# Five small edits in one diff to a two-layer network: where a row scale stands, which engine adds squares, how far apart sixteen mixing steps lie, and how weight blocks are added up

## The chip, the cores and the metric

The kernel runs on one core of a Trainium2 chip. A core has TensorE (PE, matrix products), VectorE (DVE), ScalarE (ACT), GpSimd (POOL), and SyncE (SP), which here only issues transfers; 16 DMA engines move data. ACT and POOL issue transfers as well. Each engine works through its own instructions in order and waits on semaphores for the others. The metric is device time in microseconds, the median of several executions. All arithmetic is float32: a product of two float32 matrices is made of three matmuls on a high and a low part of each operand (hi·hi, hi·lo, lo·hi), so each block of weights needs a cast (`whi`, on ACT) and a subtraction (`wlo`, on DVE) before TensorE can use it.

## The reference

512 tokens of width 2048 pass two layers. The first (forgetting attention and RWKV7) is untouched by the change. The part that matters:

```python
xn = rms_norm(h, norm_pre[1])
u, v, g = split(xn @ c_w_in[0], 3)          # 2048 x 6144
u = gelu(u); v = layer_norm(gelu(v), c_ln_g, c_ln_b)
# 16 groups of 128 channels, chunks of 128 tokens, w_s[g] is 128 x 128, lower triangle
mixed = einsum('gts,bnsgc->bntgc', w_s * causal, v_chunks) + b_s
y = (u * mixed * silu(g)) @ c_w_out[0]      # 2048 x 2048
h = h + rms_norm(y, norm_post[1])
h = h + (p[1] @ ple_w_proj[1]) * sigmoid(h @ ple_w_gate[1])   # the output
```

## The kernel before, in words

**Products of half blocks.** The large products of the second layer (`c_w_in`, `c_w_out`, the last `ple_w_gate`) are made by `seven`: a pair of column strips of 512 of W is cut into four blocks of 1024 x 512 (kh, ch), and a Strassen-like scheme makes the two strips from seven products in place of eight, each over sums of blocks. A product has eight steps k ("ticks", a counter that `tick` advances); at a step TensorE does six matmuls. `pieces` provides W's side: `load` is a plain transfer of 512 KB from SP's queue, `grow` an accumulating transfer of 512 KB from POOL's queue (it adds the block to a tile that lies in SBUF), `add` an addition on DVE (L1408). For product 4 a pair with `whole` uses `grow`; any other loads the block in half tiles of 256 KB from SP (L1445), into one of two buffers `half0`, `half1`, and adds each on DVE. `Pair` has no `whole` but the first pair of the last gate.

**Order.** For two pairs worked together (`FIRST`) the products run 1 and 2 of both, then 5, 6, 3, 4, 7 of the first, then 5, 6 and an `end` of the second: 3, 4, 7, or 4, 7, 3 in the last gate. The gating pairs of `c_w_in` go U0, G0, U1, G1, each in the order 1, 2, 5, 6, 3, 4, 7. When a product is finished, DVE combines the results (L1506 for product 3, L1519 and L1524 on for 7 and for 4 with 7) and `emit` gives each block of outputs to what follows. Work beside the products is put into a list with a due tick (`later`), and the program's order on each engine is mostly the order in which it is written, with priorities for some pieces (`high_priority`).

**Mixing.** After the values (V) and two products of a U pair, `mix` is started for eight groups, twice in all. For a group it puts into the list, relative to a tick `at`: at -11 the `load` (values `vn` and w_s, gains and shifts, from ACT's queue; the tiles are `sq`, `rstdB`, `accq`), at -4 the `norm` (ACT L1585 four times; POOL's triangle mask L1588; DVE), at 0 the `split` (a transpose on TensorE, casts L1597, L1600 and L1601), at 5 the `mul` (three matmuls L1607 on; one DVE operation on u). The group's `at` is 43 + 6.4 e for e = 0 to 7.

**c_w_out** (`last_layer`). Its outputs come in four blocks a pair; `out_block` scales each, squares it on ACT (L1141) and adds the square to `accq[e]` (L1143) for the row norm, e being the half of the tokens. Eight of these additions are on POOL and six on DVE. `row_scale(e)` (L1152, then ACT's table and L371 on) sums over partitions with TensorE and makes the row's scale; it has the highest priority. `row_scale(0)` is due in the second pair's last products, `row_scale(1)` after strip g = 0 of the following product.

**The last part.** The projection `p @ ple_w_proj` is made by `dense_tm` in four strips g of 24 matmuls; each strip's four results are copied by ACT (L1214) and parked in DRAM. Beside them `update` (L1200, L1201) adds the normed `c_w_out` result to h: half 0 in the loop, half 1 (`late`) from the first ticks of the gate's products on. Then `seven` for the gate, whose `emit` (ACT L1275, DVE L1276, L1278) makes the outputs.

Of the kernel before, what the change touches and what calls it, by code (L numbers as in the profile page):

```python
# [16 lines left out]
P = 128  # L17
# [78 lines left out]
class Pair:  # L96


    def __init__(self, W, c0, n, emit):
        self.W, self.c0, self.n, self.emit, self.whole = W, c0, n, emit, False  # L100
        self.E, self.H, self.acc, self.R, self.done = {}, {}, {}, {}, set()


class Net:
# [1017 lines left out]
    def last_layer(self, cp, fs, turn, wp, ps):  # L1122
# [8 lines left out]
        def out_block(pr, m, n, src):  # L1131
            e, q = m // 2, 2 * n + m % 2
            tl = self.slot("yh", 2 * q + e, F32) if q < 4 else self.slot("xl", 2 * q + e, F32)
            Y[q, e] = tl.rearrange("p (a t) -> p a t", a=2)
            sv = src.rearrange("p (a t) -> p a t", a=2)
            for a in range(2):
                c = 16 + 2 * q + a
                self.last = nc.scalar.activation(Y[q, e][:, a, :], sv[:, a, :], AF.Copy, scale=npost[:, c : c + 1])
            if seen[e]:
                sq = self.t(wp, [P, T], "sq")  # L1140
                nc.scalar.activation(sq, src, AF.Square)  # L1141
                eng = nc.vector if pr.n == 2 and n + e > 2 else nc.gpsimd
                eng.tensor_tensor(accq[e], accq[e], sq, ALU.add)  # L1143
            else:
                nc.scalar.activation(accq[e], src, AF.Square)
            seen[e] = True
# [60 lines left out]
        for g in range(4):  # L1207
            accs = self.dense_tm(i["ple_w_proj"][1], g * T, T, phi, plo, ps)
            for q in (g, g + 4):
                update(q, 0)  # L1210
            self.part(self.A11, g, H[g, 0])
            for m in range(4):
                pj = self.slot("xl", 4 * (g % 2) + m, F32)
                nc.scalar.copy(pj, accs[m])  # L1214
                nc.sync.dma_start(self.pd[:, m, g * T : (g + 1) * T], pj)
            x2(g)
            if g == 0:
                row_scale(1)

        pj, res = {}, {}  # L1220
# [62 lines left out]
        W = i["ple_w_gate"][1]  # L1283
        pairs = [Pair(W, 2 * j * T, 2 * j, emit) for j in range(2)]
        pairs[0].whole = True
        self.seven(FIRST(*pairs, (4, 7, 3)), Sets(nxt), ps)
        self.clock += 100
        self.tick()
# [100 lines left out]
    def pieces(self, pr, prod, keep):  # L1389
# [20 lines left out]
        for j in range(4):  # L1410
            done = None
            if prod == 1:
                tl = load(0, 0, j)
                if keep:
                    pr.E[j] = tl
                else:
                    done = tl
            elif prod == 5:
                if j not in pr.E:
                    pr.E[j] = load(0, 0, j)  # L1420
                tl = pr.E[j]
                grow(tl, 0, 1, j)
            elif prod == 2:
                tl = done = load(1, 0, j)
            elif prod == 6:
                pr.H[j] = load(1, 1, j)
                tl = pr.E[j]
                add(tl, pr.H[j])
            elif prod == 3:
                if j in pr.H:  # L1430
                    tl = pr.H[j]
                else:
                    tl = done = load(1, 1, j)
            elif prod == 7:
                tl = done = pr.H.pop(j)
                grow(tl, 0, 1, j)
            elif pr.whole:
                tl = done = pr.E.pop(j)
                grow(tl, 1, 0, j)
            else:  # L1440
                tl = done = pr.E.pop(j)
                for a in range(2):
                    g = self.t(self.wq, [P, T], f"half{a}")
                    k = 8 + 2 * j + a
                    nc.sync.dma_start(g, pr.W[k * P : (k + 1) * P, pr.c0 : pr.c0 + T])  # L1445
                    add(tl[:, a * T : (a + 1) * T], g)
# [11 lines left out]
    def seven(self, order, sets, ps, after=lambda n: None, fm=False):  # L1458
# [3 lines left out]
        for step, (pr, prod, keep) in enumerate(order):  # L1462
# [30 lines left out]
            for m in range(2):  # L1493
# [9 lines left out]
                    u2 = pr.R[1][:, m]  # L1503
                    nc.vector.tensor_tensor(u2, a, u2, ALU.add)
                elif prod == 3:
                    nc.vector.scalar_tensor_tensor(a, a, -1.0, pr.R[1][:, m], ALU.mult, ALU.subtract)  # L1506
                    pr.emit(pr, m, pr.n + 1, a)
            pr.done.add(prod)
            if prod == 7:
                u3 = pr.R[7] = pr.R[1] if 3 in pr.done else self.t(self.rp, [P, 2, T], "comb")  # L1510
                for m in range(2):
                    nc.vector.tensor_tensor(u3[:, m], acc[m], pr.R[1][:, m], ALU.add)
                    c22 = pr.R[5][:, m]
                    nc.vector.tensor_tensor(c22, c22, u3[:, m], ALU.add)
                    pr.emit(pr, 2 + m, pr.n + 1, c22)
            if prod in (4, 7) and {4, 7} <= pr.done:
                for m in range(2):
                    u = pr.R[7][:, m]
                    nc.vector.tensor_tensor(u, pr.acc[4][m], u, ALU.subtract)  # L1519
                    pr.emit(pr, 2 + m, pr.n, u)  # L1520
            after(step)

    def add_sq(self, accq, src, n, wp):
# [11 lines left out]
    def layer_c(self, cp, sets, accq, after, wp, ps):  # L1535
# [79 lines left out]
        V = [Pair(W, D + 2 * j * T, 2 * j, vals) for j in range(2)]  # L1615
        U = [Pair(W, 2 * j * T, 2 * j, gates) for j in range(2)]
        G = [Pair(W, 2 * D + 2 * j * T, 2 * j, silu) for j in range(2)]
        order = FIRST(*V)
        for pr in (U[0], G[0], U[1], G[1]):
            order += [(pr, prod, True) for prod in NEXT]  # L1620
# [30 lines left out]
        def done(step):  # L1651
# [20 lines left out]
            for j in range(2):  # L1672
                if step == nv + 14 * j + 1:
                    for e in range(8):
                        mix(8 * j + e, 5 * 8 + 3 + int(6.4 * e))
            if step == nv + 13:
                for n in range(2):
                    self.later(4, lambda n=n: saved(n))
# [290 lines left out]
```

## Time and profile before

| | us |
|---|---|
| median of 3 executions | 2251.96 (2250.07 to 2252.22) |
| the profiled execution, its own time | 2256.05 |
| its span (first to last instruction) | 2254.3 |
| TensorE busy in it | 2211.8 (98%) |
| VectorE busy | 1556.7 (69%) |
| ScalarE busy | 1274.5 (57%) |
| GpSimd busy | 264.1 (12%) |

The stages of the second layer by the trace's time: `c_w_in` until about 1885, its mixing near 1600 to 1680 and 1800 to 1860; `c_w_out` 1885 to 2045; the projection 2048 to 2079; the last gate from there to 2246, where TensorE's last matmul ends. In rows of the timeline the first number is the start, the second the duration, then engine, line, operation, output and inputs, shapes and count; brackets hold the idle time of that engine before the row and what ended it. In rows of waits the numbers are the total in us, how often, and the longest.

### The profile page before, as it was taken

How to read it: one execution, taken by the hardware profiler on the slowest of the kernel's cores; microseconds unless marked ns; L12 is line 12 of the kernel's file. 1: busy time of each engine (PE TensorE's matmuls, PEld its weight loads, DVE VectorE, ACT ScalarE, POOL GpSimd, SP SyncE). 2: the span in 40 equal slices, each digit the busy share in tenths (PEclk: the TensorE clock that was granted, in tenths of full speed). 3: DMA queues.
4: the chain of work that ended last, by engine and by line, in shares of the span. 5: the costliest groups of instructions: out<-in, count | busy, mean ns of one | idle time of the engine just before them, and what ended most of it. 6: DMA issues, size and time to landing. Idle time of an engine off the chain costs nothing.

```text
span 2254.3 us, 40541 instructions
## 1 busy us (share of the span) xinstructions
PE 2211.8 (98%) x15369; PEld 1839.4 (82%) x15369; DVE 1556.7 (69%) x3006; ACT 1274.5 (57%) x2597; POOL 264.1 (12%) x316
## 2 busy tenths in 40 slices
PE   8999999999999999999999999999999999998998
PEld 7878888888887788878888888888878879997876
DVE  8766667666633878883227356987787787989867
ACT  5545555555543677763335456656665667656744
POOL 2000010001100000000010012010110110220120
PEclk9999999999999999999999999999999999999999
DMA  7322232222324633343335345687866966577694
GB/s 235 92 79 70 74 87 82 66 76 76 85 75 116 193 103 99 103 117 129 96 103 163 121 131 143 171 212 195 214 170 181 225 177 167 137 192 246 169 260 141
DMA packets 294769, 313.79 MB, mean 139 GB/s; under 512 B 15101, under 2 KB 190878, under 8 KB 293550
## 3 DMA queue, kind: packets, MB, share of 16 engines
q1 hardware_dynamic: 249838, 253.52, 36.6%
q0 software_dynamic: 22848, 44.05, 11.3%
q10 hardware_dynamic: 21888, 13.64, 2.1%
q8 instruction: 121, 1.98, 0.4%
q14 instruction: 74, 0.61, 0.1%
HBM read 280.45 MB, written 30.70 MB: 138 GB/s over the span
## 4 chain that ended last, share of the span: by engine, by line
PE 78%; DVE 9%; DMA 6%; ACT 4%; issue 3%; SPq 0%; ACTq 0%; DVEq 0%; POOLq 0%
PE mm L1488 21%; PE mm L210 11%; PE mm L212 10%; PE mm L211 10%; PE mm L992 4%; PE mm L994 4%; PE mm L993 4%; DVE wlo L1453 3%; DMA sq<-vd 2%; PE tm L548 1%; ACT whi L1452 1%; DMA rq<-in_ple_w_gate_dram 1%; DVE rq L1408 1%; PE tm L569 1%; DMA gz<-gd 1%
## 5 line engine op out<-in xcount | busy, mean ns | idle before, releaser
L196 DVE TENSOR_TENSOR wlo<-raw,whi 128x512 fp32r<-128x512 f32 x400 | 283.5, 717 | 300.9 <-ACT whi L194 266.1
L194 ACT CAST whi<-raw 128x512 fp32r<-128x512 f32 x400 | 247.3, 619 | 349.0 <-PE mm L211 143.8
L211 PE MATMUL mm<-xl,whi 128*128 128x512 f32 x1056 | 414.5, 392 | 0.0
L210 PE MATMUL mm<-xh,whi 128*128 128x512 f32 x992 | 411.8, 415 | 0.0
L212 PE MATMUL mm<-xh,wlo 128*128 128x512 f32 x992 | 391.8, 395 | 0.0
L1452 ACT CAST whi<-rq 128x512 fp32r<-128x512 f32 x432 | 264.8, 620 | 194.1 <-PE mm L1488 120.5
L1453 DVE TENSOR_TENSOR wlo<-rq,whi 128x512 fp32r<-128x512 f32 x432 | 298.4, 700 | 103.0 <-ACT whi L1452 101.2
L211 PEld LDWEIGHTS mm<-xl,whi 128*128 128x128 f32 x1056 | 199.2, 189 | 32.4
L212 PEld LDWEIGHTS mm<-xh,wlo 128*128 128x128 f32 x992 | 186.2, 188 | 41.2
L210 PEld LDWEIGHTS mm<-xh,whi 128*128 128x128 f32 x992 | 186.9, 188 | 33.1
L1488 PE MATMUL mm<-whi,xl 128*128 128x512 f32 x512 | 165.6, 398 | 2.0 <-ACT whi L1452 1.7
L1488 PE MATMUL mm<-whi,yl 128*128 128x512 f32 x512 | 164.1, 394 | 0.4 <-ACT whi L1452 0.3
L1488 PE MATMUL mm<-whi,yh 128*128 128x512 f32 x512 | 161.4, 391 | 0.0
L1488 PEld LDWEIGHTS mm<-whi,xl 128*128 128x128 f32 x512 | 98.0, 191 | 23.5 <-ACT whi L1452 2.1
L1488 PEld LDWEIGHTS mm<-whi,yl 128*128 128x128 f32 x512 | 96.0, 188 | 21.2 <-ACT whi L1452 1.2
L1488 PEld LDWEIGHTS mm<-whi,yh 128*128 128x128 f32 x512 | 96.1, 188 | 20.2
L1453 DVE TENSOR_TENSOR wlo<-raw,whi 128x512 fp32r<-128x512 f32 x128 | 89.0, 697 | 33.6 <-ACT whi L1452 33.2
L1452 ACT CAST whi<-raw 128x512 fp32r<-128x512 f32 x128 | 78.5, 619 | 50.5 <-PE mm L1488 27.8
L1488 PE MATMUL mm<-wlo,xl 128*128 128x512 f32 x256 | 101.8, 398 | 3.0 <-DVE wlo L1453 3.0
L1488 PE MATMUL mm<-wlo,yl 128*128 128x512 f32 x256 | 100.5, 393 | 3.1 <-DVE wlo L1453 3.0
L1488 PE MATMUL mm<-wlo,yh 128*128 128x512 f32 x256 | 99.8, 390 | 0.0
L1488 PE MATMUL mm<-whi,xh 128*128 128x512 f32 x256 | 80.3, 390 | 0.0
(523 smaller groups left out, 4675.2 us busy)
## 6 DMA issues: line engine op xcount, KB each, us to landing
raw<-in_ab_w_in_dram SPq DMA_DIRECT2D x128, 512.0 KB, 3.9
rq<-in_c_w_in_dram SPq DMA_DIRECT2D x50, 512.0 KB, 5.0
raw<-in_ple_w_gate_dram SPq DMA_DIRECT2D x42, 512.0 KB, 3.9
rq<-in_c_w_in_dram POOLq DMA_DIRECT2D x36, 512.0 KB, 7.6
raw<-in_ab_w_out_dram SPq DMA_DIRECT2D x32, 512.0 KB, 3.8
raw<-in_c_w_in_dram SPq DMA_DIRECT2D x26, 512.0 KB, 5.1
half<-in_c_w_in_dram SPq DMA_DIRECT2D x48, 256.0 KB, 3.2
rq<-in_c_w_out_dram SPq DMA_DIRECT2D x24, 512.0 KB, 10.7
```

What stands on the lines that cost most here:

```text
L194: nc.scalar.copy(hi[:, : m * n], src)
L196: self.weng.tensor_tensor(lo[:, : m * n], src, f(hi[:, : m * n]), ALU.subtract)
L210: nc.tensor.matmul(acc, hi, xhi[k], start=(k == 0), stop=False)
L211: nc.tensor.matmul(acc, hi, xlo[k], start=False, stop=False)
L212: nc.tensor.matmul(acc, lo, xhi[k], start=False, stop=(k == nk - 1))
L548: nc.tensor.matmul(px[dst, e, :], a[src, e, :], b[src, e, :], start=True, stop=True)
L992: nc.tensor.matmul(accs[j], hi[:, js], xhi[k], start=(k == 0), stop=False)
L993: nc.tensor.matmul(accs[j], hi[:, js], xlo[k], start=False, stop=False)
L994: nc.tensor.matmul(accs[j], lo[:, js], xhi[k], start=False, stop=(k == nk - 1))
L1452: self.cast = nc.scalar.copy(hi, src)
L1453: nc.vector.tensor_tensor(lo, src, f(hi), ALU.subtract)
L1488: nc.tensor.matmul(o, x, y, start=(first and r == 0 and j == 0 and not a), stop=(r == 7 and j == 2), **more)
```

## The change

Line numbers of the changed kernel are one higher than before from line 101 on and 18 or 20 higher behind the combination code. The diff has six parts. `row_scale(1)` is asked for after strip 2 of the projection, not 0. All additions of squares in `out_block` go to DVE. The G pairs get `whole`: product 4's second block comes by four accumulating transfers of 512 KB a pair from POOL's queue, in place of eight half tiles and eight DVE additions. The mixing's ticks become 38 + 7.1 e. The last gate's second pair loads its half tiles into eight slots of `yl` that its product 5 has freed, in place of the two buffers. In `seven`, where product 3 is the last, products 4 and 7 are combined as each of them ends (two copies by ACT are new), and the operations on the last product's results get high priority.

```diff
@@ class Pair
-        self.W, self.c0, self.n, self.emit, self.whole = W, c0, n, emit, False
+        self.W, self.c0, self.n, self.emit = W, c0, n, emit
+        self.whole, self.half = False, None
@@ out_block
-                eng = nc.vector if pr.n == 2 and n + e > 2 else nc.gpsimd
-                eng.tensor_tensor(accq[e], accq[e], sq, ALU.add)
+                nc.vector.tensor_tensor(accq[e], accq[e], sq, ALU.add)
@@ last_layer
             x2(g)
-            if g == 0:
+            if g == 2:
                 row_scale(1)
@@ last_layer
         pairs[0].whole = True
+        pairs[1].half = lambda k: self.slot("yl", 8 + k, F32)
@@ pieces
                 for a in range(2):
-                    g = self.t(self.wq, [P, T], f"half{a}")
+                    g = pr.half(2 * j + a) if pr.half else self.t(self.wq, [P, T], f"half{a}")
@@ seven
                 elif prod == 3:
-                    nc.vector.scalar_tensor_tensor(a, a, -1.0, pr.R[1][:, m], ALU.mult, ALU.subtract)
-                    pr.emit(pr, m, pr.n + 1, a)
+                    with tc.high_priority(HP) if step == len(order) - 1 else nullcontext():
+                        nc.vector.scalar_tensor_tensor(a, a, -1.0, pr.R[1][:, m], ALU.mult, ALU.subtract)
+                        pr.emit(pr, m, pr.n + 1, a)
             pr.done.add(prod)
-            if prod == 7:
-                u3 = pr.R[7] = pr.R[1] if 3 in pr.done else self.t(self.rp, [P, 2, T], "comb")
+            if prod == 4 and 7 not in pr.done:
+                if 3 not in pr.done:
+                    for m in range(2):
+                        c22, u = pr.R[5][:, m], pr.R[1][:, m]
+                        nc.vector.tensor_tensor(c22, c22, u, ALU.add)
+                        nc.vector.tensor_tensor(acc[m], acc[m], u, ALU.subtract)
+            elif prod == 7 and 3 not in pr.done:
+                for m in range(2):
+                    c22 = pr.R[5][:, m]
+                    nc.vector.tensor_tensor(c22, acc[m], c22, ALU.add)
+                    pr.emit(pr, 2 + m, pr.n + 1, c22)
+                c21 = self.t(self.rp, [P, 2, T], "comb")
+                for m in range(2):
+                    nc.scalar.copy(c21[:, m], acc[m])
+                    nc.vector.tensor_tensor(c21[:, m], pr.acc[4][m], c21[:, m], ALU.subtract)
+                    pr.emit(pr, 2 + m, pr.n, c21[:, m])
+            elif prod == 7:
+                u3 = pr.R[7] = pr.R[1]
...
-            if prod in (4, 7) and {4, 7} <= pr.done:
-                for m in range(2):
-                    u = pr.R[7][:, m]
-                    nc.vector.tensor_tensor(u, pr.acc[4][m], u, ALU.subtract)
-                    pr.emit(pr, 2 + m, pr.n, u)
+                if 4 in pr.done:
+                    for m in range(2):
+                        u = u3[:, m]
+                        nc.vector.tensor_tensor(u, pr.acc[4][m], u, ALU.subtract)
+                        pr.emit(pr, 2 + m, pr.n, u)
@@ layer_c
         G = [Pair(W, 2 * D + 2 * j * T, 2 * j, silu) for j in range(2)]
+        for pr in G:
+            pr.whole = True
@@ layer_c
-                        mix(8 * j + e, 5 * 8 + 3 + int(6.4 * e))
+                        mix(8 * j + e, 38 + int(7.1 * e))
```

On TensorE, where the second row scale stands, before (`whi`, `wlo` are a weight block's parts, `yl` the operand's; each `mm` is a PSUM bank, and 22559 is the last bank of strip 0, 22622 and 22623 the first two of strip 1):

```order
L251 MATMUL mm_22559<-whi_22578,yl_4534_21951 128x512
L252 MATMUL mm_22559<-wlo_22579,yl_4534_21951 128x512
L253 MATMUL mm_22559<-whi_22578,yl_4535_21952 128x512
L1152 MATMUL mm_22616<-rstdB_12775,ones_118 128x256 x2
L251 MATMUL mm_22622<-whi_22628,yl_4530_21940 128x512
L252 MATMUL mm_22622<-wlo_22629,yl_4530_21940 128x512
L253 MATMUL mm_22622<-whi_22628,yl_4531_21941 128x512
L251 MATMUL mm_22623<-whi_22628,yl_4530_21940 128x512
```

and changed (22579 is the last bank of strip 1, 22636 to 22639 are the banks of strip 2):

```order
L253 MATMUL mm_22579<-wlo_22599,yl_4518_21911 128x512
L254 MATMUL mm_22579<-whi_22598,yl_4519_21912 128x512
L252 MATMUL mm_22636<-whi_22642,yl_4514_21900 128x512
L253 MATMUL mm_22636<-wlo_22643,yl_4514_21900 128x512
...
L252 MATMUL mm_22638<-whi_22642,yl_4514_21900 128x512
L253 MATMUL mm_22638<-wlo_22643,yl_4514_21900 128x512
L254 MATMUL mm_22638<-whi_22642,yl_4515_21901 128x512
L252 MATMUL mm_22639<-whi_22642,yl_4514_21900 128x512
L1152 MATMUL mm_22696<-rstdB_12775,ones_118 128x256 x2
L253 MATMUL mm_22639<-wlo_22643,yl_4514_21900 128x512
L254 MATMUL mm_22639<-whi_22642,yl_4515_21901 128x512
```

The row scale's two matmuls moved behind strip 1 and the first ten matmuls of strip 2.

On SP, the queue of plain transfers, in the second pair of the last gate, before (`rq` and `raw` are blocks of W of 512 KB, `out` the outputs):

```order
L1400 DMA rq_5010_24081<-in_ple_w_gate_dram 128x2x512
L1445 DMA half_5024_24137<-in_ple_w_gate_dram 128x512
L1445 DMA half_5025_24140<-in_ple_w_gate_dram 128x512
L1280 DMA out_dram<-yl_4874_23485 128x512
L1445 DMA half_5030_24163<-in_ple_w_gate_dram 128x512
L1445 DMA half_5031_24166<-in_ple_w_gate_dram 128x512
L1445 DMA half_5036_24189<-in_ple_w_gate_dram 128x512
L1445 DMA half_5037_24192<-in_ple_w_gate_dram 128x512
L1400 DMA rq_5061_24320<-in_ple_w_gate_dram 128x2x512
```

and changed:

```order
L1401 DMA rq_4994_24041<-in_ple_w_gate_dram 128x2x512
L1446 DMA yl_5001_24068<-in_ple_w_gate_dram 128x512
L1446 DMA yl_5002_24071<-in_ple_w_gate_dram 128x512
L1446 DMA yl_5008_24097<-in_ple_w_gate_dram 128x512
L1446 DMA yl_5009_24100<-in_ple_w_gate_dram 128x512
L1446 DMA yl_5014_24123<-in_ple_w_gate_dram 128x512
L1446 DMA yl_5015_24126<-in_ple_w_gate_dram 128x512
L1446 DMA yl_5020_24149<-in_ple_w_gate_dram 128x512
L1446 DMA yl_5021_24152<-in_ple_w_gate_dram 128x512
L1280 DMA out_dram<-yl_4858_23445 128x512
L1401 DMA rq_5045_24284<-in_ple_w_gate_dram 128x2x512
```

Eight loads now stand in one run into eight tiles, ahead of the output.

On POOL, in the first G pair, before (AFFINE_SELECT is the triangle mask of a group, here of e = 3 to 7 and of the second half's first; the transfers are those of product 7):

```order
L1588 AFFINE_SELECT accq_17942<-accq_17942 128x128
L1588 AFFINE_SELECT rstdB_12775<-rstdB_12775 128x128
L1588 AFFINE_SELECT accq_18139<-accq_18139 128x128
L1588 AFFINE_SELECT rstdB_12775<-rstdB_12775 128x128
L1404 DMA raw_18150<-in_c_w_in_dram 128x2x512
L1404 DMA raw_18173<-in_c_w_in_dram 128x2x512
L1404 DMA rq_3757_18210<-in_c_w_in_dram 128x2x512
L1588 AFFINE_SELECT accq_18324<-accq_18324 128x128
L1404 DMA rq_3763_18238<-in_c_w_in_dram 128x2x512
L1588 AFFINE_SELECT rstdB_12775<-rstdB_12775 128x128
```

and changed (masks of e = 3 to 7; the four `rq_36..` transfers behind the third mask are product 4's, the rest again product 7's):

```order
L1606 AFFINE_SELECT accq_17905<-accq_17905 128x128
L1606 AFFINE_SELECT rstdB_12775<-rstdB_12775 128x128
L1606 AFFINE_SELECT accq_18118<-accq_18118 128x128
L1405 DMA rq_3659_17784<-in_c_w_in_dram 128x2x512
L1405 DMA rq_3665_17818<-in_c_w_in_dram 128x2x512
L1405 DMA rq_3671_17845<-in_c_w_in_dram 128x2x512
L1405 DMA rq_3680_17876<-in_c_w_in_dram 128x2x512
L1405 DMA raw_18155<-in_c_w_in_dram 128x2x512
L1606 AFFINE_SELECT rstdB_12775<-rstdB_12775 128x128
L1405 DMA raw_18187<-in_c_w_in_dram 128x2x512
L1606 AFFINE_SELECT accq_18331<-accq_18331 128x128
L1405 DMA rq_3757_18210<-in_c_w_in_dram 128x2x512
```

Product 4's four transfers were added behind the mask of e = 5, and the masks of e = 6 and 7 now stand among product 7's transfers.

On DVE the last operations changed order: between the two subtractions of the last product 3 (L1506, now L1508) five other operations stood before, and two stand now.

## The prediction

> **What bounds the kernel now.** I began with the page's busy line, to see whether anything but TensorE can set the time, and then asked for TensorE's waits alone.
>
> ```profile
> span 2254.3 us, 40541 instructions
> PE 2211.8 (98%) x15369; PEld 1839.4 (82%) x15369; DVE 1556.7 (69%) x3006; ACT 1274.5 (57%) x2597; POOL 264.1 (12%) x316
> ```
>
> ```profile
> PE mm L1488 <- DVE wlo L1453: 10.2, 14, 2.3
> PE mm L1152 <- issue: 5.8, 1, 5.8
> PE mm L1607 <- DVE sg L1601: 2.4, 2, 1.9
> ```
>
> TensorE is busy for all but 42.5 us (2254.3 - 2211.8). The change keeps the count of matmuls, so it can win only idle time of TensorE, time in which its clock was lowered, and what follows the last matmul. The three rows hold 18.4 us of that idle time, and each is a place that the change touches. I then read these places one by one in the timeline and in windows of 4 us, where a window is: span, busy time of PE, PEld, DVE, ACT, POOL, granted clock, DMA share, GB/s. Everything else is layer A, which stays.
>
> **Part 1: the second row scale.** `row_scale(1)` (L1152) is queued on TensorE straight behind the first strip of the projection, and needs the last VectorE addition of squares (L1143).
>
> ```profile
> 2053.53 0.39 PE L252 MATMUL mm<-wlo,yl 128*128 128x512 f32 x1
> 2053.76 0.39 PE L253 MATMUL mm<-whi,yl 128*128 128x512 f32 x1
> 2059.97 2.04 PE L1152 MATMUL mm<-rstdB,ones 128*128 128x256 f32 x4 [5.83 <-issue]
> ```
>
> ```profile
> 2059.18 0.69 DVE L1143 TENSOR_TENSOR rstdB<-rstdB,sq 128x512 f32<-128x512 f32 x1
> ```
>
> ```profile
> 2059.06 2.03 ACT L1214 COPY xl<-mm 128x512 f32<-128x512 f32 x4
> ```
>
> ```profile
> 2056.00:2060.00 4.00, 0.03 (x1) 0.06 (x1) 3.99 (x8) 3.97 (x8) 0.00 (x0) 0.87 0.43 125
> 2060.00:2064.00 4.00, 4.00 (x10) 3.16 (x11) 3.96 (x7) 3.43 (x8) 0.00 (x0) 0.50 0.89 309
> 2064.00:2068.00 4.00, 4.00 (x15) 3.22 (x14) 3.34 (x7) 1.21 (x2) 0.00 (x0) 0.78 0.07 27
> ```
>
> The releaser "issue" is not the cause: the addition ended at 2059.87 and the matmul began at 2059.97. The stall is 5.83 us, and the clock behind it fell to 0.50 and 0.78: of these 8 us, 4 x 0.50 + 4 x 0.22 = 2.9 us are lost. At stake are 8.7 us. In the changed order 34 matmuls more stand ahead of it, the 24 of strip 1 and ten of strip 2; at 0.23 us each (the first two rows start 0.23 apart) they are 7.8 us of work that TensorE does instead of waiting 5.8, and it comes to the row scale at 2053.99 + 7.8 = 2061.8. The last addition stands one split later in VectorE's order, so it ends near 2059.87 + 0.6 = 2060.5: no wait is left there. What is late next: window 2056 to 2060 shows both VectorE (3.99 of 4) and ScalarE (3.97 of 4) full, and strip 2, which TensorE reaches 24 matmuls behind strip 0, at 2059.5, takes the PSUM banks that four copies of strip 0 on ScalarE free. They ran from 2059.06 to 2061.09, behind the last square, one every 0.5 us; the first banks are wanted half a microsecond or a whole one before they are free. I put 1.0 us on that, and 0.3 us on `update(4, 1)` (L1200), which now waits for the row scale in VectorE's queue with splits of the gate's weights behind it. Net **7.4 us** (bounds 5, when the stall moves to the copies and their 2.03 us and more stay, and 8.7).
>
> **Part 2: half tiles of the last pair.** Product 4 of the last pair takes its second block through two half tiles, loaded and added in turn.
>
> ```profile
> 2206.26 0.69 DVE L1408 TENSOR_TENSOR rq<-rq,half 128x512 f32<-128x512 f32 x1 [2.88 <-DMA half<-in_ple_w_gate_dram]
> ```
>
> ```profile
> 2207.61 0.50 PE L1488 MATMUL mm<-wlo,xl 128*128 128x512 f32 x1 [2.27 <-DVE wlo L1453]
> 2209.74 0.79 PE L1488 MATMUL mm<-wlo,xl 128*128 128x512 f32 x1 [0.46 <-DVE wlo L1453]
> ```
>
> ```profile
> 2208.00:2212.00 4.00, 3.54 (x11) 2.52 (x10) 3.61 (x6) 1.66 (x3) 0.00 (x0) 0.64 0.45 135
> 2212.00:2216.00 4.00, 4.00 (x18) 3.26 (x17) 4.00 (x8) 2.09 (x4) 0.00 (x0) 0.93 0.46 116
> ```
>
> Stalls 2.27 + 0.46, clock 4 x 0.36 + 4 x 0.07 = 1.7: 4.4 us. With eight tiles of their own no load waits for an addition of this product any more; they are issued in one run behind the loads of the products before. The eight additions stay. Against it: window 2212 to 2216 has VectorE full, so a little stays; net **4.0 us** (2.5 to 4.6).
>
> **Part 3: squares on VectorE.** Eight additions leave POOL, and VectorE gets eight of 0.69 us.
>
> ```profile
> 1970.09 7.14 DVE L1453 TENSOR_TENSOR wlo<-rq,whi 128x512 fp32r<-128x512 f32 x5 [0.31 <-ACT whi L1452]
> ```
>
> ```profile
> 1970.61 1.77 POOL L1143 TENSOR_TENSOR accq<-accq,sq 128x512 f32<-128x512 f32 x1
> ```
>
> ```profile
> 1937.50 0.39 PE L1488 MATMUL mm<-yh,wlo 128*128 128x256 f32 x1 [0.91 <-DVE wlo L1453]
> 1972.99 0.39 PE L1488 MATMUL mm<-yl,wlo 128*128 128x256 f32 x1 [0.83 <-DVE wlo L1453]
> 1975.48 0.38 PE L1488 MATMUL mm<-xh,wlo 128*128 128x256 f32 x1 [0.79 <-DVE wlo L1453]
> 2007.30 0.38 PE L1488 MATMUL mm<-yh,wlo 128*128 128x256 f32 x1 [0.46 <-DVE wlo L1453]
> ```
>
> ```profile
> 1900.00:2000.00 100.00, 96.95 (x797) 95.73 (x796) 85.59 (x123) 59.66 (x112) 21.32 (x14) 1.00 0.61 158
> ```
>
> Five splits that should take about 5 x 0.69 = 3.4 us took 7.14, just where POOL adds. Four stalls of TensorE, 3.0 us together, lie beside these additions, at full clock (1.00). They go. The price is 8 x 0.69 = 5.5 us of VectorE in a stage where it is 85.6% busy, part of it inflated by POOL itself: hidden on average by the 14.4 us left there, but an addition ahead of a split can delay that split by 0.69. I allow for 1 us: net **2 us** (-1, when four of the eight delay TensorE by 0.69 and more, to 3.0).
>
> **Part 4: the end.** Products 4 and 7 are combined early, and product 3's result gets priority. Before, VectorE ended thus:
>
> ```profile
> 2244.55 0.69 DVE L1506 SCALAR_TENSOR_TENSOR mm<-mm,comb 128x512 f32<-128x512 f32 x1
> 2245.15 1.28 DVE L1276 TENSOR_TENSOR comb<-comb,xh 128x512 f32<-128x512 f32 x2
> 2246.35 1.28 DVE L1278 TENSOR_TENSOR yl<-yl,comb 128x512 f32<-128x512 f32 x2
> 2247.55 0.69 DVE L1276 TENSOR_TENSOR mm<-mm,xh 128x512 f32<-128x512 f32 x1
> 2248.15 0.69 DVE L1506 SCALAR_TENSOR_TENSOR mm<-mm,comb 128x512 f32<-128x512 f32 x1
> 2250.22 0.69 DVE L1278 TENSOR_TENSOR xh<-xh,mm 128x512 f32<-128x512 f32 x1
> ```
>
> Five operations, at 0.60 from start to start, stand between the first L1506 and the second. Afterwards two do, so the second comes 1.8 us sooner; one leftover addition moves behind it, 0.6. Two copies on ScalarE are new (a copy of this size above: 2.03 / 4 = 0.5 us each), under product 3's matmuls. Net **1.2 us** (0.5 to 1.5).
>
> **Part 5: mixing and the third block of `c_w_in`.** Here the unknown is widest.
>
> ```profile
> 1640.00:1660.00 20.00, 18.34 (x79) 14.04 (x78) 20.00 (x32) 14.71 (x28) 3.07 (x2) 1.00 0.21 60
> 1804.00:1820.00 16.00, 15.13 (x68) 12.10 (x67) 15.57 (x23) 11.88 (x22) 0.60 (x1) 1.00 0.54 157
> 1820.00:1824.00 4.00, 2.12 (x9) 1.39 (x8) 2.98 (x6) 0.62 (x1) 0.00 (x0) 0.93 0.64 215
> 1824.00:1828.00 4.00, 4.00 (x14) 3.10 (x13) 3.48 (x6) 1.25 (x3) 0.00 (x0) 0.64 0.69 212
> 1840.00:1844.00 4.00, 2.08 (x9) 1.19 (x7) 0.86 (x3) 2.66 (x7) 0.00 (x0) 0.99 1.08 203
> 1844.00:1848.00 4.00, 4.00 (x13) 3.26 (x14) 3.58 (x7) 3.31 (x8) 2.05 (x2) 0.58 0.53 121
> ```
>
> ```profile
> 1841.34 0.88 ACT L1585 ACTIVATE sq<-sq,nb,rv 128x128 f32<-128x128 f32 x2 [5.15 <-DMA sq<-vd]
> ```
>
> ```profile
> rq<-in_c_w_in_dram POOLq DMA_DIRECT2D x18, 512.0 KB, 7.0
> half<-in_c_w_in_dram SPq DMA_DIRECT2D x22, 256.0 KB, 3.1
> ```
>
> Idle: 1.66 + 0.87 + 1.88 + 1.92 = 6.3 us; clock: 4 x (0.36 + 0.42) = 3.1; at stake 9.4. Two causes show: VectorE full (20.00 of 20), and ScalarE, which works in order, held 5.15 us by the load of a group's values. The change takes 16 additions of 0.60 us off VectorE in these stages, 9.6 us, and starts a group every 7.1 ticks in place of 6.4, its load 11 ticks ahead as before. It adds eight accumulating transfers in POOL's queue, which land after 7.0 us where a half needs 3.1 (the DMA view of 1600 to 1860), when the DMA share is already 1.08 (1840 to 1844). So VectorE's cause goes and the load's may grow. Saved at best 9.4, lost at worst a second stall like 1841's per half (1.92 + 1.7, twice: 7.2). Nearer to the upper row, since 16 additions are certain and the collisions are not: **3 us** (-7 to 9).
>
> The page "TensorE: Matmul & The Clock Gate" of the Trainium skill (Part 1, "What's actually happening") says that the half clock comes after an idle window of about 3.4 us. For the stall of 5.83 us trace and page agree; after the shorter ones here, which the page would let pass at full clock, the rows show 0.64, 0.64 and 0.58, so the measurement decides. By the page parts 2 and 5 would lose their clock terms, at most 1.7 and 1.0 us of what I count, and the time would be 2237.1; the rows leave that no chance of its own.
>
> **Sum.** 7.4 + 4.0 + 2.0 + 1.2 + 3.0 = 17.6 us. The profiled execution took 2256.05 us, so its like would take 2238.5. The median is 4.1 us below it with the same code, so I take the sum off the median: 2251.96 - 17.6 = **2234.4 us**.
>
> **Rivals.** (a) *The mixing becomes the bound.* POOL works in order, and the changed order puts the mask (L1588) of group 5 ahead of all four accumulating transfers of product 4; that mask waits for its own load. If loads are late under a full DMA, TensorE waits at product 4 and again at product 7, in both pairs: four stalls. At 8.7 us each, the price of L1152's, part 5 becomes -34.8 and the time 2251.96 - 14.6 + 34.8 = 2272. It turns the change slower once the four cost more than 14.6 + 4.5 = 19.1 us, 4.8 each. For it: DMA share 1.08, 5.15 us of a late load. Against it: a tick, one k of a product, is six matmuls, 1.4 us, and product 3 stands between the last use of those blocks and product 4: eight ticks, 11 us, for transfers that land in 7.0. Chance 0.05. (b) *The mixing gains nothing or loses some*, halfway to part 5's lower bound, -3.5: 2251.96 - 14.6 + 3.5 = 2240.9. Chance 0.20. (c) *The row scale's stall only moves*: VectorE and ScalarE are both full from 2056, so strip 2 waits for its banks instead; half of part 1 stays, 2234.4 + 3.7 = 2238.1. Chance 0.20. (d) *All mixing stalls go*: 17.6 + 6.4 = 24.0, 2228. Chance 0.15. (e) *Several parts fall short at once*, parts 1 and 3 at their lower bounds and part 5 at -7: 5 - 1 - 7 + 4.0 + 1.2 = 2.2, 2249.8. Chance 0.05. My forecast, within some 3 us: 0.35.
>
> **Range and chances.** A difference of 0.2% (4.5 us) is about what a measurement of this kernel can tell from no change. Cases (a) and (e) and a tail of (b), 0.03, are beyond 2247, and a tail of (d), 0.05, is below 2226: 2226 to 2247 leaves 0.18 out. Slower is (a), 0.05; no change is (e) with the end of (b)'s tail, 0.07; the rest is faster. So faster 0.88, same 0.07, slower 0.05.
>
> **What would show it.** L1152 (one line on the same operation) without a stall and windows there at 1.00; a stall of about a microsecond at strip 2's first matmul would be my leftover, one of 4 us rival (c). No half tile in the last product 4, and its window at 1.00. No split of 7 us in the `c_w_out` stage, and VectorE above 88% there. The second L1506 about 2 us behind the first. In the mixing, TensorE's idle time below 3 us in each half; rows of it waiting behind `rq` transfers of POOL at product 4 or 7 would be rival (a). I am wrong if the idle time of the mixing grows, or if the additions on VectorE turn up as new waits for `wlo`.

## The result, and the profile after

| | median us | ratio to before, 95% interval |
|---|---|---|
| before | 2252.12 (2248.74 to 2253.65, 12 runs) | |
| changed | 2248.02 (2243.19 to 2249.99, 12 runs) | 0.9981 (0.9972 to 0.9990) |

The change saves 4.1 us where 17.6 were forecast. One execution of e3 below (2412.68 us) and one of e4 (3012.12 us) were slow, at a lower granted clock; the ratios leave them out, and without them the medians given there would be 2249.69 and 2229.74 us. The profiled execution of the changed kernel took 2247.82 us with a span of 2245.8. The page of the changed kernel:

```profile
span 2245.8 us, 40515 instructions
PE 2209.3 (98%) x15369; PEld 1835.5 (82%) x15369; DVE 1543.0 (69%) x3000; ACT 1274.4 (57%) x2599; POOL 260.4 (12%) x316
```

TensorE's waits in the changed kernel (us in total, times, longest):

```profile
PE mm L1489 <- DVE wlo L1454: 6.5, 14, 2.3
PE mm L1489 <- ACT whi L1453: 5.6, 5, 2.3
PE mm L1625 <- DVE sg L1619: 2.5, 2, 1.3
```

The row of 5.8 us at L1152 is gone. Waits for `wlo` shrank from 10.2 to 6.5 us. New is the second row: waits for `whi`, ScalarE's casts, grew from 1.9 to 5.6 us.

To see which stage gave and which took, I cut each trace at six places: the first matmul that reads `xl` in the seven-product code (A), the last transposition of `xh` into the operand of `c_w_out` (B), the first row-scale matmul (C), the first and the last `whi`,`yl` matmul of the projection (D, E), and the last `whi`,`xl` matmul of the gate (F); then the end of the span. Each number below is the difference of two such starts, in us; C to D, left out, took 17.1 in every kernel. The first column, the start itself, differs by 4 us between kernels with the same code ahead of it.

| kernel | A at | A to B: `c_w_in`, mixing | B to C: `c_w_out` | D to E: projection | E to F: gate | F to end |
|---|---|---|---|---|---|---|
| before | 1440.1 | 455.6 | 135.7 | 30.9 | 166.7 | 8.2 |
| changed | 1441.7 | **461.7** | 130.5 | 22.6 | 164.9 | 7.3 |
| e1 mixing undone | 1438.5 | 451.9 | 131.3 | 23.1 | 164.3 | 7.3 |
| e2 old ticks | 1439.9 | 453.8 | 130.9 | 23.7 | 164.9 | 7.3 |
| e3 half tiles of G | 1439.8 | 465.6 | 130.9 | 23.2 | 164.6 | 7.3 |
| e4 norm pinned | 1440.8 | 444.4 | 129.7 | 22.7 | 164.8 | 7.3 |
| e5 early start, old spacing | 1438.6 | 450.9 | 131.3 | 22.8 | 164.5 | 7.3 |
| e6 row scale alone | 1440.5 | 455.8 | 137.1 | 22.7 | 166.9 | 8.2 |
| e7 pinned, squares on POOL | 1440.8 | 443.1 | 136.3 | 22.6 | 165.9 | 7.4 |
| e8 pinned, half buffers | 1439.9 | 442.9 | 130.7 | 22.6 | 167.3 | 7.4 |
| e9 group 1 a tick earlier | 1439.4 | 453.3 | 130.3 | 22.8 | 165.6 | 7.3 |
| e10 before, norm pinned | 1438.6 | 452.1 | 135.7 | 29.5 | 166.0 | 8.2 |
| e11 pinned, old spacing | 1437.7 | 448.6 | 129.9 | 22.6 | 164.8 | 7.3 |
| e12 pinned again | 1437.4 | 445.0 | 130.3 | 23.9 | 164.9 | 7.3 |

Every stage behind the mixing got shorter, by 5.2, 8.3, 1.8 and 0.9 us: 16.2 us. The mixing's stage got 6.1 us longer. (The profiled execution of before, 2256.05 us, lies above all its 12 timed runs. Part of that may be in its mixing: e1 and e6 have the same mixing, and their stages took 451.9 and 455.8, the latter again in the longest execution of its kernel. So by the traces the loss in the mixing is between 6 and 10 us; the timed runs below put it at 11.5.)

**The row scale** stands where it was forecast to and waits for nothing; at strip 2's first matmul 0.17 us are left, where 1.0 were allowed for. Timeline of TensorE, changed kernel:

```profile
2062.24 0.50 PE L252 MATMUL mm<-whi,yl 128*128 128x512 f32 x1 [0.17 <-ACT xl L1214]
```

**Squares.** A window of the `c_w_out` stage, first before, then changed (columns: span, busy time of PE, PEld, DVE, ACT, POOL with their instruction counts, granted clock, DMA share, GB/s):

```profile
1936.00:1940.00 4.00, 3.05 (x23) 2.64 (x22) 3.92 (x5) 3.19 (x7) 0.90 (x1) 1.00 0.00 0
```

```profile
1936.00:1940.00 4.00, 4.00 (x36) 4.00 (x35) 4.00 (x6) 1.69 (x3) 0.00 (x0) 1.00 0.00 0
```

The stall of 0.91 us that the prediction counted in this window shows as 0.95 us idle, but TensorE started 23 matmuls in place of 36. At 4.00 / 36 = 0.111 us each, 13 are 1.4 us. PEld, the weight loads, is busy for 4.00 of 4 in the changed window and for 2.64 before. Behind the stall matmuls came more slowly for a while; what slows them the runs do not show.

**The last gate** kept a stall of the same size, for another reason. Changed kernel: TensorE and VectorE, SyncE's issues of the eight half tiles, and a window.

```profile
2199.85 0.50 PE L1489 MATMUL mm<-wlo,xl 128*128 128x512 f32 x1 [2.34 <-DVE wlo L1454]
```

```profile
2198.50 0.69 DVE L1409 TENSOR_TENSOR rq<-rq,yl 128x512 f32<-128x512 f32 x1 [1.48 <-DMA yl<-in_ple_w_gate_dram]
```

```profile
2182.61 9.67 SPq L1446 DMA_DIRECT2D yl<-in_ple_w_gate_dram  x8
```

```profile
2196.00:2200.00 4.00, 1.66 (x7) 1.05 (x8) 2.19 (x4) 1.02 (x2) 0.00 (x0) 1.00 1.11 260
```

The loads no longer wait for a buffer, they are all issued by 2192.3. But the DMA engines are full (share 1.11), and the halves take 14.1 us in the median from issue to landing. Between 2180 and 2204 POOL's accumulating transfers take a share of 0.65 of the engines for 2.87 MB, SyncE's loads 0.42 for 3.37 MB. The clock stayed at 1.00 this time.

**The end** went as forecast: the second subtraction of product 3 comes 1.95 us behind the first (3.60 before). VectorE, changed kernel:

```profile
2237.17 0.69 DVE L1508 SCALAR_TENSOR_TENSOR mm<-mm,comb 128x512 f32<-128x512 f32 x1
...
2239.12 0.69 DVE L1508 SCALAR_TENSOR_TENSOR mm<-mm,comb 128x512 f32<-128x512 f32 x1
...
2241.64 0.69 DVE L1278 TENSOR_TENSOR xh<-xh,mm 128x512 f32<-128x512 f32 x1
```

**The mixing** is where the gain went. (Its second half begins earlier than the 1800 us named with the profile before: the first load of values is issued at 1763 there.) TensorE's waits between 1580 and 1880 sum to 12.2 us, 7.3 before, so the idle time of the mixing grew. The part of it that waits for VectorE's `wlo` is 3.0 us in both. TensorE's two longest stalls there, one in each half:

```profile
1614.60 0.50 PE L1489 MATMUL mm<-whi,yh 128*128 128x512 f32 x1 [2.10 <-ACT whi L1453]
...
1783.96 0.49 PE L1489 MATMUL mm<-whi,yh 128*128 128x512 f32 x1 [2.26 <-ACT whi L1453]
```

ScalarE ahead of the first of them, and the same place in the second half (ACTq L1594 issues the load of a group's values, L1596 and L1597 the loads of a group's gains and shifts, L1603 is the first use of the values):

```profile
1604.23 0.35 ACTq L1596 DMA_DIRECT2D rstdB<-in_c_ln_g_dram  x1
...
1605.12 0.34 ACTq L1597 DMA_DIRECT2D rstdB<-in_c_ln_b_dram  x1
...
1605.58 0.38 ACTq L1594 DMA_DIRECT2D sq<-vd  x1
1606.06 1.66 ACT L1453 CAST whi<-raw 128x512 fp32r<-128x512 f32 x3
1612.78 1.26 ACT L1603 ACTIVATE sq<-sq,nb,rv 128x128 f32<-128x128 f32 x3 [5.06 <-DMA sq<-vd]
...
1774.68 0.42 ACTq L1594 DMA_DIRECT2D sq<-vd  x1
...
1782.14 1.26 ACT L1603 ACTIVATE sq<-sq,nb,rv 128x128 f32<-128x128 f32 x3 [5.26 <-DMA sq<-vd]
```

Group 1's load is issued at 1605.58. Three casts follow, then the first use, at which ScalarE stands for 5.06 us until the load has landed, 7.2 us after its issue. The casts of the weights are queued behind, so TensorE runs dry. Over 1590 to 1870 ScalarE waited so for 42.7 us, where 18.2 stand for 1600 to 1860 before:

```profile
ACT sq L1603 <- DMA sq<-vd: 42.7, 16, 5.3
```

What the transfer competes with, SyncE's next issues and a window of it:

```profile
1607.59 1.57 SPq L1401 DMA_DIRECT2D raw<-in_c_w_in_dram  x2
```

```profile
1609.00:1613.00 4.00, 3.50 (x16) 2.57 (x14) 0.00 (x0) 0.22 (x1) 0.00 (x0) 1.00 1.02 383
```

Two loads of 512 KB of weights are issued from 2 us behind it, and from 1609 on all three land together while the engines move 383 GB/s. That is only the second half of the 7.2 us. In the 3 us behind the issue of the values the engines moved 37 GB/s: 227 packets of ScalarE's own queue, 0.11 MB, so half a KB each, and two packets of SyncE's. These are gains and shifts (64 KB each), by their tile those of group 2, which ScalarE had issued 1.35 and 0.46 us ahead of the values, as soon as group 0 was done with the tile. The values themselves, in packets of 2 KB, moved mostly from 3.5 to 5.5 us behind their issue, beside the weights. So the load first stood behind small packets in its own queue and then shared the engines.

No transfer of POOL is near this load, so my rival (a) does not fit; but the two traces alone do not say whether the ticks or G's accumulating transfers moved the loads.

### The profile page after: what moved, and what is told of

It reads as the page before. It is cut to its first block, busy times and chain, and to the rows that moved or that the text cites. A ratio compares the mean times of both kernels' runs of the same rounds, so it can differ in the third digit from the quotient of the medians.

```text
span 2245.8 us, 40515 instructions
## 1 busy us (share of the span) xinstructions
PE 2209.3 (98%) x15369; PEld 1835.5 (82%) x15369; DVE 1543.0 (69%) x3000; ACT 1274.4 (57%) x2599; POOL 260.4 (12%) x316
## 5 line engine op out<-in xcount | busy, mean ns | idle before, releaser
L1454 DVE TENSOR_TENSOR wlo<-rq,whi 128x512 fp32r<-128x512 f32 x432 | 292.3, 685 | 117.1 <-ACT whi L1453 115.8
## 6 DMA issues: line engine op xcount, KB each, us to landing
rq<-in_c_w_out_dram SPq DMA_DIRECT2D x24, 512.0 KB, 11.5
```

The lines of the kernel that those rows point to most:

```text
L1454: nc.vector.tensor_tensor(lo, src, f(hi), ALU.subtract)
```

## The experiments

All medians below have before's runs of the same batch beside them: 2253.58 us for e1 to e4, 2251.63 for e5 to e8, 2252.33 for e9 to e12.

### First batch: which half of part 5, and whether the load is exposed

**e1**, both edits of the mixing taken back:

```diff
-                        mix(8 * j + e, 38 + int(7.1 * e))
+                        mix(8 * j + e, 5 * 8 + 3 + int(6.4 * e))
...
-        for pr in G:
-            pr.whole = True
```

> The changed kernel with the mixing's old ticks (43 + 6.4 e) and the G pairs' half tiles back; the other parts stay. Theory (the mixing stages cost some 6 us more than before, by the two traces, and eat the gain of the rest): 2248 - 6 = 2242 us, ratio to before 0.9955. Rival (the rest gains less than its places show, and the mixing is level): 2248 us, ratio 0.998.

Measured: 2237.07 us, ratio 0.9930 (0.9917 to 0.9942). The other four parts together give 0.0070 x 2252 = 15.8 us, and part 5 costs 11.5 us (0.9981 against 0.9930; 7 to 16 by the ends of the two intervals). That is more than the theory expected; the rest is close to what the prediction summed for it (14.6).

**e2**, the first two lines of that diff alone; **e3**, the last two alone.

> The changed kernel with the old ticks alone, accumulating transfers of G kept. Theory T (the earlier first group is at fault: its load of values falls beside the four accumulating transfers of U's product 7, and ScalarE waits 3.5 us and 5 us for the first two groups in both halves): about 2242 us, stalls of 2.1 and 2.3 us at the first groups gone. Rival W (the accumulating transfers of G are at fault): 2248 us, the stalls stay.

> The changed kernel with G's half tiles back, new ticks kept. Theory T: about 2248 us or a little more, ScalarE waits for the first two groups' values as in the changed kernel. Rival W: about 2242 us.

Measured: e2 2237.99 us, ratio 0.9935 (0.9923 to 0.9947); e3 2249.71 us, ratio 0.9988 (0.9979 to 0.9997). So it is the ticks. G's accumulating transfers, with the 16 additions that they take off VectorE, change nothing that these runs can tell, neither with the old ticks (0.9935 against 0.9930) nor with the new (0.9981 against 0.9988). Rival W falls. ScalarE's wait in e3:

```profile
ACT sq L1603 <- DMA sq<-vd: 37.9, 14, 6.6
```

**e4**, the first use of a group's values tied to a later cast. In the code `load` stands 11 ticks ahead of `at` and `norm` 4, seven casts apart, but the program orders `norm`'s work by what it expects to be ready: in ScalarE's order mostly two or three casts stand between the two (one to four before, two to five in the changed kernel). The edit puts it where the ticks say:

```diff
                 for m in range(4):
-                    nc.scalar.activation(vn[:, m, :], vn[:, m, :], AF.Identity, ...)
+                    with tc.issue_after(self.cast.ins):
+                        nc.scalar.activation(vn[:, m, :], vn[:, m, :], AF.Identity, ...)
```

> The changed kernel with each group's norm held on ScalarE behind the weight cast of its own tick, so that five to seven casts (7 to 10 us) lie between a group's load and its first use in place of two or three. Theory T in its sharper form (the load is exposed since only two casts, 2.7 us, cover a landing of 4 to 7 us): ScalarE's wait for values falls from 42.7 us below 10, the mixing's TensorE stalls below 4 us in all, time 2238 to 2241 us. Rival W: no change, 2248 us, since transfers would still come late.

Measured: 2231.19 us, ratio 0.9903 (0.9888 to 0.9918), better than expected. ScalarE's wait for values and TensorE's waits in the mixing (1580 to 1880):

```profile
ACT sq L1604 <- DMA sq<-vd: 6.4, 2, 4.5
```

```profile
PE mm L1489 <- ACT whi L1453: 1.6, 1, 1.6
PE mm L1489 <- DVE wlo L1454: 0.2, 1, 0.2
```

The first group's load is issued at the same place as in the changed kernel (1593.26 there), and its first use now follows 10 us later, without a wait:

```profile
1593.15 0.39 ACTq L1594 DMA_DIRECT2D sq<-vd  x1
...
1603.19 1.26 ACT L1604 ACTIVATE sq<-sq,nb,rv 128x128 f32<-128x128 f32 x3
```

That the exposed load makes the stalls is shown: with the same ticks, the same transfers and only the cover changed, the stage goes from 461.7 to 444.4 us.

### Second batch: why the ticks, and the sizes of the other parts

**e5**, the early start with the old spacing: `38 + int(6.4 * e)`.

> The changed kernel with ticks 38 + 6.4 e: the early start kept, the spacing as before. Theory T (the early start puts the first two groups' loads beside the accumulating transfers of U's product 7): 2246 to 2250 us like the changed kernel, with ScalarE waiting 3.5 us and 5 us for the first two groups. Rival S (the wider spacing is at fault): 2238 us, like the old ticks.

Measured: 2235.26 us, ratio 0.9932 (0.9920 to 0.9945). Theory T falls: the early start costs nothing, as rival S had it. The first half of e5's mixing shows what was right in theory T and where it went wrong. ScalarE of e5:

```profile
1598.62 0.49 ACT L1603 ACTIVATE sq<-sq,nb,rv 128x128 f32<-128x128 f32 x1 [3.65 <-DMA sq<-vd]
...
1603.22 0.33 ACTq L1594 DMA_DIRECT2D sq<-vd  x1
...
1606.67 0.88 ACT L1603 ACTIVATE sq<-sq,nb,rv 128x128 f32<-128x128 f32 x2 [1.43 <-DMA sq<-vd]
```

Group 0 waits 3.65 us here too (3.54 in the changed kernel), and TensorE, which has casts in hand, loses 0.8 us by it in three pieces. Group 1's load, one cast earlier than in the changed kernel, lands in 3.45 us in place of 7.2. It is issued ahead of the load of the shifts (L1597, 1603.61 here), and not behind it.

**e6**, `if g == 0:` to `if g == 2:` ahead of `row_scale(1)`, on the kernel before, and nothing else.

> The kernel before with the row scale asked for after strip 2 and nothing else. By the two traces the projection takes 30.9 us before and 22.6 us after, so 8 us should go: ratio 0.9965, 2245 us against 2253. Rival (other parts of the change made room for it, the stall moves otherwise): half of that or less, 2249 us or more.

Measured: 2245.23 us, ratio 0.9975 (0.9965 to 0.9985): 5.6 us, interval 3.4 to 7.9. That lies between the 8 us expected and the rival's half of it, and the interval reaches the rival. By the trace the part stands by itself: it has the projection at 22.7 us and the row scale without a wait:

```profile
2061.83 0.50 PE L251 MATMUL mm<-whi,yl 128*128 128x512 f32 x1 [0.27 <-ACT xl L1214]
...
2064.35 1.07 PE L1152 MATMUL mm<-rstdB,ones 128*128 128x256 f32 x4
```

**e7** and **e8** start from e4 and take one part back each, the engine of the squares (`eng = nc.vector if pr.n == 2 and n + e > 2 else nc.gpsimd`) and the last pair's slots (the line `pairs[1].half = ...`).

> The kernel with pinned norms (2231 us) with eight additions of squares back on POOL. From the c_w_out stage (135.7 us before, 129.7 to 131.3 in all five kernels with the additions on VectorE): 5 us slower, 2236 us, and the stage at 135 us again. By the prediction's term: 2 us slower, 2233.

> The kernel with pinned norms (2231 us) with the last pair's half tiles back in two buffers. From the gate stage (166.7 us before, 164.3 to 164.9 after): 2 us slower, 2233 us. By the prediction's term: 4 us slower, 2235 us.

Measured: e7 2235.27 us, ratio 0.9930 (0.9917 to 0.9942); against e4 and e12 (0.9903, 0.9895) it is 6 to 8 us slower (the intervals of e7 and e4 just touch), and its `c_w_out` stage took 136.3 us against 129.7 and 130.3. The long run of splits is back beside POOL's additions, and so are TensorE's stalls, five of them and 5.2 us in all; the longest comes 28 us behind that run, at the end of three other additions. e7's VectorE and TensorE:

```profile
1959.17 8.34 DVE L1455 TENSOR_TENSOR wlo<-rq,whi 128x512 fp32r<-128x512 f32 x7 [0.31 <-ACT whi L1454]
```

```profile
1995.98 0.38 PE L1490 MATMUL mm<-yh,wlo 128*128 128x256 f32 x1 [1.74 <-DVE wlo L1455]
```

e8 2230.48 us, ratio 0.9911 (0.9898 to 0.9925): its interval overlaps those of e4 and e12, so by time the own slots can't be told from none. By the traces the gate takes 167.3 us in place of 164.8 and 164.9, 2.4 us. The longest stall there is 2.28 us in e8 (first row) and 1.46 us in e12 (second row), but 1.80 in e4 and 2.34 in the changed kernel, which have own slots too. What e8's has besides is a lowered clock, 0.88 and 0.69 in the two windows of 4 us from 2180 on:

```profile
2182.26 0.50 PE L1488 MATMUL mm<-wlo,xl 128*128 128x512 f32 x1 [2.28 <-DVE wlo L1453]
```

```profile
2185.93 0.50 PE L1489 MATMUL mm<-wlo,yh 128*128 128x512 f32 x1 [1.46 <-DVE wlo L1454]
```

### Third batch: one tick of one group, and what the cover is worth elsewhere

**e9**, the changed kernel with `38 + int(7.1 * e) - 1 * (e == 1)`: group 1 at tick 44, all others as they were.

> The changed kernel with one number changed: group e = 1 starts at tick 44 in place of 45, in both halves. Theory P (formed after the early start with the old spacing came out fast: a group's load is covered by two casts only, and lands in 3.5 us or in 7 us by where it falls among SP's loads of weights; in the changed kernel group 1's load of 256 KB shares the DMA engines with two loads of 512 KB issued 2 to 3.6 us behind it): ScalarE's wait for group 1 falls from 5.1 and 5.3 us to about 1.5, the stalls of 2.1 and 2.3 us behind it go, 4 to 6 us saved, 2243 us. Rival S (it is the spacing as such, over all groups): under 1.5 us saved, 2247 us.

Measured: 2237.99 us, ratio 0.9941 (0.9928 to 0.9955). One tick of one group in each half is worth 9 us (0.9981 against 0.9941; 4 to 14 by the ends of the intervals), by the medians more than the 4 to 6 expected, and most of the 11.5 us that part 5 had cost. In all ScalarE still waits 35.5 us for values in e9 (42.7 in the changed kernel): most of this wait costs TensorE nothing. What went is its wait for `whi`, 0.3 us in the mixing of e9 in place of 5.6, and with it the two long stalls. ScalarE and SyncE of e9 at the place:

```profile
1602.65 0.33 ACTq L1594 DMA_DIRECT2D sq<-vd  x1
...
1603.05 0.42 ACTq L1597 DMA_DIRECT2D rstdB<-in_c_ln_b_dram  x1
1603.54 1.14 ACT L1453 CAST whi<-raw 128x512 fp32r<-128x512 f32 x2
1605.93 0.88 ACT L1603 ACTIVATE sq<-sq,nb,rv 128x128 f32<-128x128 f32 x2 [1.25 <-DMA sq<-vd]
```

```profile
1605.07 3.37 SPq L1401 DMA_DIRECT2D raw<-in_c_w_in_dram  x2
```

The load lands in 3.3 us and ScalarE waits 1.25 us for it; the weights' loads are issued from 2.4 us behind it over 3.4 us, one by one, where they came within 1.6 us of each other in the changed kernel. Rival S falls as a rule for the whole table: the other fourteen groups have their wide spacing and cost little.

The expectation put the slow landing down to these two loads of weights alone. The tick moved something else as well: the load of the values now stands ahead of that of the shifts (L1597) in ScalarE's queue, and in the 3 us behind its issue this queue moved 0.33 MB, where it moved 0.11 in the changed kernel. Over both halves the landings of group 1 fall into three sorts. Ahead of the shifts it lands in 3.3 to 3.9 us (e5, e9). Behind them it takes 4.5 to 4.8 us with the old ticks (before, e1, e2), though there too two loads of 512 KB are issued about 1.5 us behind it, and 6.6 to 7.5 us in the changed kernel and e3. So the two loads of weights alone do not make 7 us; the order in ScalarE's own queue counts, and what fills the engines when the values' turn comes. I did not move either of them alone, so what each is worth is not shown.

**e10**, e4's edit on the kernel before.

> The kernel before with norms held behind the weight cast of their own tick and nothing else. By theory P the old kernel's mixing has the same exposure (18.2 us of ScalarE's wait), but with groups 6.4 ticks apart the later groups' loads wait for a buffer and keep only two to four casts of cover: half of the gain, c_w_in stage from 455.6 to about 449 us, 2246 us against 2252, ratio 0.997. Rival S: none of it, 2252.

Measured: 2251.37 us, ratio 1.0000 (0.9991 to 1.0009). This missed. The load's wait did fall, and the stall moved: TensorE's waits in the mixing sum to 7.3 us as before, but now it waits for the split of a group's values (`sg`) at the group's own products, three times and 5.5 us in all (2.4 before). That norms which are held back come late for this table would explain it. The spacing of 6.4 ticks alone is not it, for e11 below has the same spacing from tick 38 on and no wait for `sg`; I did not try it apart. ScalarE's and TensorE's waits of e10:

```profile
ACT sq L1586 <- DMA sq<-vd: 8.2, 4, 4.2
```

```profile
PE mm L1608 <- DVE sg L1602: 5.5, 3, 2.1
```

**e11**, e4 with `38 + int(6.4 * e)`, and **e12**, e4 once more.

> The kernel with pinned norms with ticks 38 + 6.4 e in place of 38 + 7.1 e. Theory P: the first five groups covered, groups 5 and 6 with three and one casts: c_w_in stage 446 to 449 us against 444.4, 2 to 4 us slower than the pinned kernel, 2233 to 2235 us. Rival S (wide spacing costs): faster than the pinned kernel.

> The kernel with pinned norms once more, beside the one with the old spacing: 2231 us, ratio 0.990, c_w_in stage 443 to 445 us.

Measured: e11 2229.98 us, ratio 0.9906 (0.9892 to 0.9919); e12 2227.53 us, ratio 0.9895 (0.9882 to 0.9909). By time the two can't be told apart; the stage took 448.6 us in e11 against 445.0 and 444.4, and ScalarE waited twice as long for values (e11; 6.5 us in e12):

```profile
ACT sq L1604 <- DMA sq<-vd: 12.8, 3, 6.1
```

So the wider spacing, which went with 11 us of loss beside an exposed load (the changed kernel against e5), is no loss once the load has its cover. The 4 us that it gains by these traces are no more than the stages of one and the same mixing differ by above (451.9 and 455.8), so a gain is not shown. e12, the changed kernel with one more line, is the fastest of all, 1.05% (0.91 to 1.18) below before.

## Why the prediction was wrong, point by point

- **Part 1, the row scale: right.** 7.4 us were forecast; the stage gave 8.3 in the trace, 5.6 (3.4 to 7.9) by time alone (e6). The wait for the copies' banks, put at 1.0, measured 0.17 us in the changed kernel and 1.5 us at most (e12), so rival (c), half of part 1, did not come.
- **Part 2, the last gate: right in kind, half in size.** 4.0 forecast, 1.8 to 2.4 by the traces, just below the lower bound. The step that failed is that the loads, once free of the buffers, would be in time: they were issued in time and landed late, since the DMA share stood at 1.10 to 1.11 from 2176 to 2200. The stall stayed (2.34 us, for 2.27 and 0.46); what was won is, by my estimate, the 1.7 us of clock that had been lost behind it (0.64 and 0.93 before, 1.00 now). The forecast looked at what the loads waited for and not at whether their bytes had room.
- **Part 3, the squares: right in kind, too small.** 2.0 forecast with 3.0 as the upper bound, 5.2 in the two traces and 6.0 to 6.6 in e7's stage. Two steps failed. Four stalls were priced by their idle time, 3.0 us. TensorE's rows of this stage show six, 4.3 us, before and one, 1.0 us, in the changed kernel, so 3.3 us of idle time went; the other 1.9 us are, by my estimate, matmuls that come more slowly behind a stall, for the windows above count 1.4 us of lost matmuls for 0.95 idle. And the 1 us set aside for additions ahead of splits was not taken: the one stall left (at 2019.70) stands where one of 0.92 us stood before.
- **Part 4, the end: right**, 0.9 for 1.2.
- **Part 5, the mixing: wrong, and it decides.** +3 us forecast with -7 as the lower bound; it cost 11.5. The step that failed is "its load 11 ticks ahead as before". The 11 and 4 ticks are where the code asks for the work. In ScalarE's order mostly two or three casts lie between a group's load and its first use, 2.8 to 4.2 us at a tick's 1.4, while the rows I quoted gave the wait (5.15 us) and neither the lead nor the landing (8.3 us behind the issue, with one cast between). With too little cover, each group's wait is what its transfer happens to meet, and a new table of ticks draws all sixteen anew. In the changed kernel group 1 came behind group 2's gains and shifts in ScalarE's queue and then met two loads of 512 KB, in both halves, since both have the same table. The bound of -7 came from doubling one seen stall and had no such draw in it. A second step failed with it, that VectorE's cause goes: the 16 additions taken off VectorE and the accumulating transfers, on which I spent rival (a), are neutral together (e2, e3), and TensorE waited for `wlo` as long as before (3.0 us).
- **Of the rivals**, none had the mechanism. The time landed between (b), 2240.9, and (e), 2249.8, and 1 us outside the range; the price of (b), "loses some", was the right direction for the wrong reason.
- **The clock rule.** The page "TensorE: Matmul & The Clock Gate" of the Trainium skill (Part 1, "What's actually happening") puts the half clock behind an idle window of about 3.4 us. The changed kernel's two stalls of 2.10 and 2.26 us were followed by these windows:

```profile
1616.00:1620.00 4.00, 4.00 (x13) 3.10 (x13) 2.97 (x5) 1.37 (x3) 0.00 (x0) 0.64 0.55 164
1784.00:1788.00 4.00, 3.77 (x16) 2.83 (x17) 4.00 (x7) 2.92 (x6) 0.00 (x0) 1.00 0.20 47
```

The shorter one lost clock and the longer did not. So I was right that stalls below 3.4 us can cost clock, and wrong to book 1.7 us of it for every new one.

## What to carry to other kernels

A lead written in the code is not a lead on the chip: before moving work that begins with a load, count in the order of the engine that uses it how many instructions lie between the issue and the first use, and hold that against the landing times in the trace, the long ones too. Look also at what stands ahead of the load in its own queue. If the cover is shorter than the landing, fix the cover first (here one line, 17 us of the stage, though the same line on the kernel before was worth nothing); until then any shift of the table draws new collisions, and one tick of one group was worth 9 us. And price a stall by the instructions that were not started, not by the idle time alone, and a transfer that is freed from a buffer by the room on the DMA engines at its new place.

## What the runs showed of the hardware that I had not expected

- The same transfer of 256 KB, issued by ScalarE, landed in 3.3 us (e9), 3.45 us (e5) and 7.2 us (changed kernel) within 3 us of the same place of the program. In the last case the 256 KB moved mostly from 3.5 us behind the issue on, when two loads of 64 KB issued ahead of them on the same queue, in packets of half a KB, were through.
- Beside plain loads, POOL's accumulating transfers took more of the engines for fewer bytes: a share of 0.65 for 2.87 MB against 0.42 for 3.37 MB (changed kernel, 2180 to 2204).
- Where PEld is busy for 4.00 of 4 without a stall, a window with 0.95 us of idle time had 13 matmuls fewer, 1.4 us.
- The granted clock after stalls of about 2 us is not set by their length: 0.64 after 2.10 us and 1.00 after 2.26 us in one execution; 1.00 in e1 after this one:

```profile
1839.46 0.50 PE L1489 MATMUL mm<-whi,xl 128*128 128x512 f32 x1 [1.96 <-ACT whi L1453]
```

```profile
1842.00:1846.00 4.00, 4.00 (x22) 3.25 (x21) 3.83 (x7) 3.37 (x9) 2.00 (x2) 1.00 0.61 107
```
